# Feed-forward blocks: P6 of the first block ahead of four row casts, and the sums of gated rows behind the next quarter products' additions

## The chip, the core and the metric

The kernel runs on one core of one Trainium2 chip. The metric is device time in microseconds (us) of one execution; the kernel before takes 1314.16 us, the median of 3 runs (1312.84 to 1315.1). The engines are named as in the profile: PE is TensorE's matrix multiplication and PEld its weight loads, DVE is VectorE, ACT is ScalarE, POOL is GpSimd, SP is the engine that issues most DMAs.

## The reference

One layer of a hybrid encoder over 1024 tokens of width 1024: two attention branches, gated, and then a SwiGLU feed-forward part of hidden width 2816. All data are float32. The change touches the feed-forward part alone:

```
x = x + y @ W_out                                   # end of the attention part
h = rms_norm(x, norm_ffn)
u = silu(h @ w_gate) * (h @ w_up)                   # 2816 hidden columns = 22 blocks of 128
x = x + u @ w_down
```

## The kernel before, in words

**Three products for one.** Each float32 operand is split into a high half and a low half of the type fp32r (`split`, lines 48 to 55: a cast on ACT, line 50, then a subtraction on DVE, line 51; or, with a scale, lines 53 and 54). A product is made of three matrix multiplications, high by high, high by low and low by high: lines 823, 824 and 825.

**Seven products for eight.** Large products go through a Strassen-Winograd scheme (`Seven`). A 2 by 2 block product takes seven products P1 to P7 instead of eight, of sums of the blocks. A step P works in one of four PSUM banks of its set: P1 and P2 in bank X, P5 in V, P6 and P3 in Y, P7 and P4 in Z. There are two sets of banks, and the blocks of hidden columns take them in turn: even blocks (bankX_6627, bankY_6628, bankV_6629, bankZ_6630) and odd blocks (bankX_6631, bankY_6632, bankV_6633, bankZ_6634). After P1 ACT copies bank X into bank Y, and after P6 bank Y into bank Z (line 827), since the later products add onto those values. So P6 waits for the copy into Y, and P7 for the copy into Z. A sum of weight blocks is made on DVE (line 805), cast on ACT and completed on DVE before its product, as part of `prepare`.

**The order on the engines.** On PE the order is the order of the program everywhere. From `begin` (line 1202) to `change.close()` (line 1406) the order of ACT and DVE is also that of the program: this stretch is the passage from the attention part to the feed-forward part. Outside it a scheduler orders ACT, DVE, POOL and SP ahead of time, bound by the data and by `tc.issue_after(x)`, which keeps what is written under it behind instruction x. Each engine then works through its own list in order.

**The passage.** Blocks 0 and 1 (generators `ga` and `gb` over `hidden`, order `LAST2` = 1, 5, 6, 7, 3, 2, 4) are worked alternately while the rows of x are still being summed, split and cast (`feed`, `prepare_ffn`). After both P6, `ffn_norm` transposes the sums of squares on PE (line 1226) into the two V banks, DVE reduces them (lines 1228 and 1229), POOL takes the power -0.5 (line 1230). After both P7, `spread_norm` spreads the two results over the partitions by PE transposes (line 156), which need POOL's results. P3 follows.

**The pairs.** From block 4 on two blocks are worked as a pair. P1 of both is made together by a quarter-sized scheme of seven products (`first_products`) in the X and V banks, and parts of their P5 are worked between these products. In it DVE adds the fifth quarter product twice: into the odd block's bank X (line 1330) and into the even block's bank X (line 1333). Then ACT copies the even block's bank X into its bank Y (line 1334, on which the even block's P6 waits), and after the fourth quarter product the odd block's (line 1339). While this goes on the pair before is completed on DVE: normalised and gated (`gated`: lines 1239 to 1241; lines 1360 to 1366), and its rows u are summed for the last product (`keep` and `TokenSums`, lines 837, 840, 841 and 853, tiles ta and tb, in the profile tau and tbu), and seven tiles of a pair are stored to DRAM (line 1379, on SP). `keep` is called as the odd block of a pair is completed, in the middle of the next pair's `first_products`.

Of the kernel before, what the change touches and what calls it, by code (L numbers as in the profile page):

```python
# [25 lines left out]
def block_kernel(ctx, tc, x, xt, small, w_in, rpb, t5, w_ba, w_bb, w_out, w_gate, w_up, w_down,  # L26
                 onehot, swmask, namask, out):
    nc = tc.nc
# [196 lines left out]
    att = {}  # L225
# [205 lines left out]
    def run(gen):  # L431
        for _ in gen:
            pass
# [809 lines left out]
    us = {}  # L1243

    def quarter_rows():

        base = [temp2(f"q{z}").rearrange("p (m h t) -> p m h t", m=2, h=2) for z in "ab"]
        for j in range(4):
            dst = base[j // 2][:, j % 2]
            nc.sync.dma_start(dst, x1_dram[tok(2 * j), LO].rearrange("p (h t) -> p h t", h=2))  # L1250
        for _ in range(3):
            yield
        for j in range(4):
            dst = base[j // 2][:, j % 2]
# [12 lines left out]
        for args in ((5, t1, b12, b11, ALU.subtract), (6, t2, t1, b22, ALU.subtract),  # L1267
                     (7, b12, b12, b22, ALU.subtract), (4, b21, b21, t2, ALU.add)):
            yield
            put(*args)  # L1270
            yield
# [10 lines left out]
    def first_products(a, b):  # L1282
# [47 lines left out]
        nc.vector.tensor_add(xb[:, Q1], xb[:, Q1], p5)  # L1330
        multiply(2)
        multiply(3)
        nc.vector.tensor_add(xa[:, Q1], xa[:, Q1], p5)
        nc.scalar.copy(a.banks["Y"], xa)  # L1334
        b.step(5, (3,))
        (w[4],) = parts("d", a22, 256)
# [1 line left out]
        multiply(4)  # L1338
        att["first"] = nc.scalar.copy(b.banks["Y"], xb).ins
        yield  # L1340

    def hidden(i, order=ORDER, given=()):

        s = hid[i]
        us[i] = scratch2(f"u{i}")
        sg_lo, sg_hi = halves(us[i])
        p5, c22 = halves(scratch2(f"p5{i}"))
        y, z, v = (s.banks[b] for b in "YZV")
        for p in order:
            if p not in given:  # L1350
                s.step(p)
            if p == 2:
                gated(sg_lo, s.banks["X"], 0)
            elif p == 5:
                with ExitStack() as line:
                    if given:
                        line.enter_context(tc.issue_after(att["first"]))
                    nc.scalar.copy(p5, v)
            elif p == 7:
                att["two"] = nc.vector.tensor_add(c22, z, p5).ins  # L1360
            elif p == 3:
                nc.vector.tensor_add(sg_hi, y, p5)
                gated(sg_hi, sg_hi, 1)
            elif p == 4:
                nc.vector.tensor_mul(sg_lo, z, sg_lo)
                att["two"] = nc.vector.tensor_mul(sg_hi, c22, sg_hi).ins
                if i % 2:
                    keep(i // 2, us[i - 1], us[i])
            if p == order[3]:
                prefetch_ffn(i + 2)  # L1370
            yield p

    def keep(k, u0, u1):

        (b11, b12), (b21, b22) = halves(u0), halves(u1)
        t = TokenSums(f"u{k}", b11, b12, b22).rest(b21)
        for n, p in enumerate(ORDER):
            row = (7 * k + n) * P
            nc.sync.dma_start(u_dram[row:row + P, :], t[p][0])
# [11 lines left out]
    for i, g in enumerate((ga, gb)):  # L1391
        prepare_ffn((i, 7))
        next(g)
    add_up_ffn(4)
    feed(*((3, j) for j in range(4)))
    for i, g in enumerate((ga, gb)):
        prepare_ffn((i, 3))
        next(g)
    rs = [ffn_norm(half, sets[half]["V"]) for half in range(2)]
    feed(*((4, j) for j in range(4)))  # L1400
    both_blocks()
# [3 lines left out]
    feed(*((5, j) for j in range(4)))  # L1405
    change.close()
    in_turn(ga, gb)
    pieces = quarter_rows()
    for _ in hidden(2):
        next(pieces)  # L1410
# [5 lines left out]
    for i in range(4, NF, 2):  # L1416

        first = first_products(hid[i], hid[i + 1])
        next(first)
        run(g)  # L1420
        run(first)
        ga, g = (hidden(i + a, ORDER[1:], (5,)) for a in range(2))
        for p in ORDER[1:]:
            next(ga)
            if p != 4:
                next(g)
    run(g)

    acc = [big.tile([P, T], F32, tag="H", name=f"acc{m}", bufs=16) if m < 4 else scratch2(f"acc{m}")
           for m in range(8)]  # L1430
# [100 lines left out]
```

## Time and profile before

| what | value |
|---|---|
| median of 3 runs | 1314.16 us (1312.84 to 1315.1) |
| the profiled execution | 1314.27 us, span from first to last instruction 1312.4 us |
| PE busy in the span | 1301.0 us, 99% |
| DVE, ACT, POOL busy | 1014.9, 695.0 and 180.4 us |
| PE idle by named waits, feed-forward part | 0.9 us and 0.6 us |
| clock granted to TensorE | 1.000 |

The time of an execution is the span and what lies around it, 1.87 us here. PE is busy almost all the time, so what counts is where PE does not start its next matrix multiplication when it could. In the rows of a timeline the columns are: start in us from the span's start, duration in us, engine, line of the kernel, operation, output<-input, shape, count, and in brackets the idle time before with what ended it. A row of the chain that ended last has start, duration, engine, tile and line.

### The profile page before, as it was taken

How to read it: one execution, taken by the hardware profiler on the slowest of the kernel's cores; microseconds unless marked ns; L12 is line 12 of the kernel's file. 1: busy time of each engine (PE TensorE's matmuls, PEld its weight loads, DVE VectorE, ACT ScalarE, POOL GpSimd, SP SyncE). 2: the span in 40 equal slices, each digit the busy share in tenths (PEclk: the TensorE clock that was granted, in tenths of full speed). 3: DMA queues.
4: the chain of work that ended last, by engine and by line, in shares of the span. 5: the costliest groups of instructions: out<-in, count | busy, mean ns of one | idle time of the engine just before them, and what ended most of it. 6: DMA issues, size and time to landing. Idle time of an engine off the chain costs nothing.

```text
span 1312.4 us, 19559 instructions
## 1 busy us (share of the span) xinstructions
PE 1301.0 (99%) x6594; PEld 1130.9 (86%) x6594; DVE 1014.9 (77%) x2025; ACT 695.0 (53%) x1459; POOL 180.4 (14%) x321
## 2 busy tenths in 40 slices
PE   9999999999999999999999999999999999999998
PEld 8999999999888888888888888888888888888887
DVE  5678867776687758878999878887777799697774
ACT  7567867776664324636456544443444455363532
POOL 1364645564320000000000000000000000000000
PEclk9999999999999999999999999999999999999999
DMA  9532424242435348756774533233233356672532
GB/s 327 132 89 60 107 67 109 61 134 56 146 117 184 122 153 267 238 185 225 238 251 121 169 105 108 90 101 117 88 100 121 121 176 217 243 246 65 185 128 81
DMA packets 180997, 191.92 MB, mean 146 GB/s; under 512 B 21104, under 2 KB 126576, under 8 KB 180896
## 3 DMA queue, kind: packets, MB, share of 16 engines
q1 hardware_dynamic: 180640, 190.57, 46.3%
q8 instruction: 52, 0.85, 0.3%
q14 instruction: 49, 0.40, 0.1%
q10 hardware_dynamic: 256, 0.10, 0.0%
HBM read 133.19 MB, written 52.37 MB: 141 GB/s over the span
## 4 chain that ended last, share of the span: by engine, by line
PE 88%; DMA 5%; DVE 3%; ACT 2%; SPq 1%; issue 1%; POOL 1%; ACTq 0%; DVEq 0%; POOLq 0%
PE bankZ L823 6%; PE bankZ L824 6%; PE bankZ L825 6%; PE bankY L823 6%; PE bankY L824 6%; PE bankY L825 6%; PE bankX L823 4%; PE bankX L825 4%; PE bankX L824 4%; PE pj L324 4%; PE pj L325 4%; PE pj L326 4%; PE o L648 3%; PE bankV L824 3%; PE bankV L823 3%; PE bankV L825 3%
## 5 line engine op out<-in xcount | busy, mean ns | idle before, releaser
L602 ACT ACTIVATE E<-E,nm 128x384 f32<-128x384 f32 (+3 forms) x128 | 75.7, 592 | 47.4 <-DVE nm L596 41.3
L604 POOL TENSOR_SCALAR E<-E,nm 128x384 f32<-128x384 f32 (+1 forms) x128 | 73.4, 574 | 94.6 <-DVE nm L603 72.8
L51 DVE TENSOR_TENSOR pl<-tp,ph 128x384 fp32r<-128x384 f32 (+1 forms) x128 | 66.5, 519 | 17.6 <-ACT ph L50 16.5
L50 ACT CAST ph<-tp 128x384 fp32r<-128x384 f32 (+1 forms) x128 | 57.4, 448 | 21.3 <-PE tp L614 20.7
L50 ACT CAST f<-f 128x512 fp32r<-128x512 f32 x87 | 50.9, 620 | 23.7 <-DMA f<-u_dram 23.3
L51 DVE TENSOR_TENSOR f<-f 128x512 fp32r<-128x512 f32 x87 | 56.4, 691 | 7.1 <-ACT f L50 7.0
L614 PE MATMUL tp<-ident,E 128*128 128x128 f32 x352 | 59.5, 272 | 0.9 <-POOL E L604 0.9
L614 PEld LDWEIGHTS tp<-ident,E 128*128 128x128 f32 x352 | 45.2, 140 | 5.9 <-POOL E L604 1.2
L344 POOL TENSOR_TENSOR ss<-ss,mhalf 128x4 f32<-128x4 f32 (+2 forms) x42 | 49.7, 1182 | 3.2
L648 PE MATMUL o<-pl,v 128*128 128x256 f32 (+2 forms) x160 | 48.7, 305 | 0.9 <-DVE pl L51 0.8
L603 DVE RECIPROCAL nm<-nm 128x1 f32<-128x1 f32 x128 | 20.4, 161 | 36.8 <-ACT E L602 35.4
L648 PE MATMUL o<-ph,v 128*128 128x256 f32 (+2 forms) x160 | 45.9, 301 | 0.4 <-ACT ph L50 0.4
L590 PE MATMUL s<-k,q 128*128 128x384 f32 (+1 forms) x128 | 46.0, 359 | 0.0
L1230 POOL TENSOR_TENSOR rs<-rs,mhalf 128x4 f32<-128x4 f32 x2 | 2.2, 1105 | 318.3 <-DVE rs L1229 318.3
L591 PE MATMUL s<-k,q 128*128 128x384 f32 (+1 forms) x128 | 41.3, 323 | 0.0
L596 DVE CUSTOM_DVE_ANT_0 E<-s,bsw,cols 128x384 f32<-128x384 f32 (+1 forms) x64 | 37.0, 577 | 4.5 <-PE s L591 3.8
L1240 ACT ACTIVATE u<-u 128x512 f32<-128x512 f32 x44 | 27.5, 630 | 22.4 <-DVE u L1239 22.2
L596 DVE CUSTOM_DVE_ANT_0 E<-s,bna 128x384 f32<-128x384 f32 (+1 forms) x64 | 33.0, 517 | 4.2 <-PE s L591 3.8
L50 ACT CAST f_5h<-s1f 128x512 fp32r<-128x512 f32 x22 | 13.7, 622 | 41.7 <-DVE s1f L805 36.4
L823 PE MATMUL bankY<-f,f_6h 128*128 128x512 f32 x88 | 34.5, 392 | 0.9 <-ACT bankY L1334 0.9
L823 PE MATMUL bankZ<-f,f_7h 128*128 128x512 f32 x88 | 34.4, 390 | 0.6 <-ACT bankZ L827 0.6
L824 PE MATMUL bankV<-f,f_5h 128*128 128x512 f32 x88 | 34.4, 391 | 0.0
(1266 smaller groups left out, 4648.0 us busy)
## 6 DMA issues: line engine op xcount, KB each, us to landing
f<-u_dram SPq DMA_DIRECT2D x77, 256.0 KB
wg_s<-in_w_gate_dram SPq DMA_DIRECT2D x22, 512.0 KB
u_dram<-u SPq DMA_DIRECT2D x33, 256.0 KB
o_dram<-of SPq DMA_DIRECT2D x32, 256.0 KB
o<-o_dram SPq DMA_DIRECT2D x32, 256.0 KB
sg<-g_dram SPq DMA_DIRECT2D x32, 256.0 KB
g_dram<-go SPq DMA_DIRECT2D x24, 256.0 KB
u_dram<-tau SPq DMA_DIRECT2D x22, 256.0 KB
```

Of the source, the lines that this page charges most:

```text
L50: a = nc.scalar.copy(hi, src)
L51: b = (eng or nc.vector).tensor_tensor(lo, src, f(hi), ALU.subtract)
L324: nc.tensor.matmul(ps[:, :384], lh, his[k][:, :384], start=(k == 0), stop=False)
L325: nc.tensor.matmul(ps[:, :384], lh, los[k][:, :384], start=False, stop=False)
L596: att["bound"] = nc.vector.tensor_tensor_reduce(E[:, :n], s[:, :n], hd["bias"](qb), -1.0, sk if sw else 1e30, ALU.add, ALU.min, nm[:, 0:1] ...
L602: nc.scalar.activation(E[:, :m], E[:, :m], AF.Exp, bias=nm[:, 0:1], scale=-1.0, accum_out=nm[:, 1:2])
L604: nc.gpsimd.tensor_scalar(E[:, :n], E[:, :n], nm[:, 1:2], 1.0, op0=ALU.mult, op1=ALU.mult)
L614: nc.tensor.transpose(tp[:, tok(j)], hd["E"][qq][:, ko:ko + P], ident)
L648: nc.tensor.matmul(hd["O"][half][:, (a - half * 4) * P:(z + 1 - half * 4) * P], v[:, kb].rearrange("p a e -> p (a e)"), pp[:, (a - q0) * P ...
L823: nc.tensor.matmul(ps, hi[:, tok(j)], bh, start=first, stop=False, skip_group_check=True)
L824: nc.tensor.matmul(ps, hi[:, tok(j)], bl, start=False, stop=False, skip_group_check=True)
L825: nc.tensor.matmul(ps, lo[:, tok(j)], bh, start=False, stop=end, skip_group_check=True)
```

## The change

It has two parts. In the passage, the first block's P6, with its copy of bank Y into bank Z, is written ahead of the casts and subtractions of the rows of P3 (`feed` of `(3, j)`), and the weights of P3 are prepared for both blocks in one call after them. In the pairs, `keep` is no longer called where the odd block is completed: it is put on a list, and for the pairs in the middle it is called after the next pair's `first_products`, under `tc.issue_after(att["put"])`, where `att["put"]` is the addition of line 1333. For the first pair and the last one it is called directly after their blocks end, which is where it was.

```
--- before.py
+++ after.py
@@ -1330,7 +1330,7 @@
         nc.vector.tensor_add(xb[:, Q1], xb[:, Q1], p5)
         multiply(2)
         multiply(3)
-        nc.vector.tensor_add(xa[:, Q1], xa[:, Q1], p5)
+        att["put"] = nc.vector.tensor_add(xa[:, Q1], xa[:, Q1], p5).ins
         nc.scalar.copy(a.banks["Y"], xa)
         b.step(5, (3,))
         (w[4],) = parts("d", a22, 256)
@@ -1338,6 +1338,8 @@
         multiply(4)
         att["first"] = nc.scalar.copy(b.banks["Y"], xb).ins
         yield
+
+    done_rows = []
 
     def hidden(i, order=ORDER, given=()):
 
@@ -1365,7 +1367,7 @@
                 nc.vector.tensor_mul(sg_lo, z, sg_lo)
                 att["two"] = nc.vector.tensor_mul(sg_hi, c22, sg_hi).ins
                 if i % 2:
-                    keep(i // 2, us[i - 1], us[i])
+                    done_rows.append(lambda: keep(i // 2, us[i - 1], us[i]))
             if p == order[3]:
                 prefetch_ffn(i + 2)
             yield p
@@ -1391,11 +1393,11 @@
     for i, g in enumerate((ga, gb)):
         prepare_ffn((i, 7))
         next(g)
+    next(ga)
     add_up_ffn(4)
     feed(*((3, j) for j in range(4)))
-    for i, g in enumerate((ga, gb)):
-        prepare_ffn((i, 3))
-        next(g)
+    prepare_ffn((0, 3), (1, 3))
+    next(gb)
     rs = [ffn_norm(half, sets[half]["V"]) for half in range(2)]
     feed(*((4, j) for j in range(4)))
     both_blocks()
@@ -1405,6 +1407,7 @@
     feed(*((5, j) for j in range(4)))
     change.close()
     in_turn(ga, gb)
+    done_rows.pop()()
     pieces = quarter_rows()
     for _ in hidden(2):
         next(pieces)
@@ -1419,12 +1422,15 @@
         next(first)
         run(g)
         run(first)
+        with tc.issue_after(att["put"]):
+            done_rows.pop()()
         ga, g = (hidden(i + a, ORDER[1:], (5,)) for a in range(2))
         for p in ORDER[1:]:
             next(ga)
             if p != 4:
                 next(g)
     run(g)
+    done_rows.pop()()
 
     acc = [big.tile([P, T], F32, tag="H", name=f"acc{m}", bufs=16) if m < 4 else scratch2(f"acc{m}")
            for m in range(8)]
```

Below, the order of the engines as it is built: line, operation, output<-input with the buffers' numbers, shape. First ACT in the passage, before. Here p is the copy of a bank V, f_0 to f_2 and f_3_8046 are the row casts of P3, f_3h the casts of the two blocks' P3 weights, bankZ<-bankY the copies after P6.

```order
L1358 COPY p_8155<-bankV_6629 128x512
L50 CAST f_7h<-s3f_7954 128x512
L1358 COPY p_8170<-bankV_6633 128x512
L50 CAST f_0_8040<-f_0_8040 128x512
L50 CAST f_1_8042<-f_1_8042 128x512
L50 CAST f_2_8044<-f_2_8044 128x512
L50 CAST f_3_8046<-g22x_8104 128x512
L50 CAST f_3h<-s4f_7849 128x512
L827 COPY bankZ_6630<-bankY_6628 128x512
L50 CAST f_3h<-s4f_7955 128x512
L827 COPY bankZ_6634<-bankY_6632 128x512
```

The same place now:

```order
L1360 COPY p_8155<-bankV_6629 128x512
L50 CAST f_7h<-s3f_7954 128x512
L1360 COPY p_8170<-bankV_6633 128x512
L827 COPY bankZ_6630<-bankY_6628 128x512
L50 CAST f_0_8040<-f_0_8040 128x512
L50 CAST f_1_8042<-f_1_8042 128x512
L50 CAST f_2_8044<-f_2_8044 128x512
L50 CAST f_3_8046<-g22x_8104 128x512
L50 CAST f_3h<-s4f_7849 128x512
L50 CAST f_3h<-s4f_7955 128x512
L827 COPY bankZ_6634<-bankY_6632 128x512
```

The first block's copy (bankZ_6630) has moved ahead of four row casts and one weight cast; the second block's copy has stayed where it was. On DVE and PE nothing has moved in the passage.

Second, DVE at the pair of blocks 6 and 7, before. The tiles u_8903 and u_8906 are the rows of the pair 4 and 5, tau and tbu their sums, f_6l, f_2l and f_7l low halves of weights, s2f and s3f sums of weights, qpf the fifth quarter product. The remaining sum, line 837, stands five rows ahead of this piece.

```order
L1366 TENSOR_TENSOR u_8906<-p_8907,u_8906 128x512
L840 TENSOR_TENSOR tau_9126<-tau_9126,u_8906 128x512
L841 TENSOR_TENSOR tbu_9127<-u_8903,u_8906 128x512
L51 TENSOR_TENSOR f_6l<-s2f_9032,f_6h 128x512
L51 TENSOR_TENSOR f_2l<-wg_s,f_2h 128x512
L853 TENSOR_TENSOR tbu_9127<-u_8906,tau_9126 128x512
L1330 TENSOR_TENSOR bankX_6631<-bankX_6631,qpf_9169 128x256
L51 TENSOR_TENSOR f_2l<-wg_s,f_2h 128x512
L805 TENSOR_TENSOR s3f_9007<-wu__9002,wg_s 128x512
L1333 TENSOR_TENSOR bankX_6627<-bankX_6627,qpf_9169 128x256
L51 TENSOR_TENSOR f_7l<-s3f_9007,f_7h 128x512
```

The same place now:

```order
L51 TENSOR_TENSOR f_6l<-s2f_9032,f_6h 128x512
L51 TENSOR_TENSOR f_2l<-wg_s,f_2h 128x512
L1330 TENSOR_TENSOR bankX_6631<-bankX_6631,qpf_9156 128x256
L51 TENSOR_TENSOR f_2l<-wg_s,f_2h 128x512
L805 TENSOR_TENSOR s3f_9007<-wu__9002,wg_s 128x512
L1333 TENSOR_TENSOR bankX_6627<-bankX_6627,qpf_9156 128x256
L837 TENSOR_TENSOR tau_9220<-u_8903 128x512
L841 TENSOR_TENSOR tbu_9221<-u_8903,u_8906 128x512
L51 TENSOR_TENSOR f_7l<-s3f_9007,f_7h 128x512
L805 TENSOR_TENSOR s3f_9033<-wu__9028,wg_s 128x512
L840 TENSOR_TENSOR tau_9220<-tau_9220,u_8906 128x512
L853 TENSOR_TENSOR tbu_9221<-u_8906,tau_9220 128x512
```

The four sums have gone from ahead of the two additions into bank X (lines 1330 and 1333) to behind both of them, and the product of line 1366 (now 1368) has moved two rows ahead. The pairs 8 to 21 have the same move, with small changes beside it: on ACT one cast of the even block's f_6h stands behind the copy of line 1317, and the copies into Z stand one cast earlier. On SP the seven stores of a pair keep their place between the weight loads; among them the two of u_8906 now stand ahead of the first of tau. PE's order is the same in both kernels.

More of the change, by code (lines that the diff above doesn't have):

```diff
@@ L1332, in first_products @@
         multiply(3)
-        nc.vector.tensor_add(xa[:, Q1], xa[:, Q1], p5)
+        att["put"] = nc.vector.tensor_add(xa[:, Q1], xa[:, Q1], p5).ins
         nc.scalar.copy(a.banks["Y"], xa)
@@ L1340, in first_products @@
         yield
+    done_rows = []
     def hidden(i, order=ORDER, given=()):
@@ L1367, in hidden @@
                 if i % 2:
-                    keep(i // 2, us[i - 1], us[i])
+                    done_rows.append(lambda: keep(i // 2, us[i - 1], us[i]))
             if p == order[3]:
@@ L1393, in block_kernel @@
         next(g)
+    next(ga)
     add_up_ffn(4)
     feed(*((3, j) for j in range(4)))
-    for i, g in enumerate((ga, gb)):
-        prepare_ffn((i, 3))
-        next(g)
+    prepare_ffn((0, 3), (1, 3))
+    next(gb)
     rs = [ffn_norm(half, sets[half]["V"]) for half in range(2)]
@@ L1407, in block_kernel @@
     in_turn(ga, gb)
+    done_rows.pop()()
     pieces = quarter_rows()
@@ L1421, in block_kernel @@
         run(first)
+        with tc.issue_after(att["put"]):
+            done_rows.pop()()
         ga, g = (hidden(i + a, ORDER[1:], (5,)) for a in range(2))
@@ L1427, in block_kernel @@
     run(g)
+    done_rows.pop()()
     acc = [big.tile([P, T], F32, tag="H", name=f"acc{m}", bufs=16) if m < 4 else scratch2(f"acc{m}")
```

## The prediction

> **What bounds the kernel now.** I read the page first, then the waits of PE, then the timeline at the two places that the waits name.
>
> ```profile
> span 1312.4 us, 19559 instructions
> PE 1301.0 (99%) x6594; PEld 1130.9 (86%) x6594; DVE 1014.9 (77%) x2025; ACT 695.0 (53%) x1459; POOL 180.4 (14%) x321
> ```
>
> PE is busy in all but 11 us of the span. Its instructions and their order are the same in both kernels, so the change can only give back time in which PE stood still, or make it stand longer. These are the named waits of PE from 690 us to the end (total us, times, longest):
>
> ```profile
> PE bankY L823 <- ACT bankY L1334: 0.9, 1, 0.9
> PE bankZ L823 <- ACT bankZ L827: 0.6, 1, 0.6
> ```
>
> Two waits, once each: the first block's P7 behind its copy into Z (the first part of the change), and one even block's P6 behind its copy into Y (the second part). In the eight other pairs that copy is in time, so there the second part has nothing to win.
>
> **First part, the passage.** PE, then ACT, then DVE and POOL:
>
> ```profile
> 692.42 0.39 PE L825 MATMUL bankY<-f,f_6l 128*128 128x512 f32 x1
> ...
> 695.37 1.04 PE L1226 MATMUL bankV<-ident,wide_rs 128*128 128x128 f32 x8
> 697.00 0.50 PE L823 MATMUL bankZ<-f,f_7h 128*128 128x512 f32 x1 [0.59 <-ACT bankZ L827]
> 697.34 0.39 PE L824 MATMUL bankZ<-f,f_7h 128*128 128x512 f32 x1
> ```
> ```profile
> 693.72 1.66 ACT L50 CAST f<-f 128x512 fp32r<-128x512 f32 x3
> 695.28 0.62 ACT L50 CAST f<-g22x 128x512 fp32r<-128x512 f32 x1
> 695.84 0.62 ACT L50 CAST f_3h<-s4f 128x512 fp32r<-128x512 f32 x1
> 696.37 0.58 ACT L827 COPY bankZ<-bankY 128x512 f32<-128x512 f32 x1
> ```
> ```profile
> 696.32 1.89 DVE L51 TENSOR_TENSOR f<-f 128x512 fp32r<-128x512 f32 x3
> ...
> 698.73 1.29 DVE L51 TENSOR_TENSOR f_3l<-s4f,f_3h 128x512 fp32r<-128x512 f32 x2
> 699.93 0.69 DVE L1228 TENSOR_REDUCE rs<-bankV 128x4 f32<-128x512 f32 x1
> ...
> 700.97 2.18 POOL L1230 TENSOR_TENSOR rs<-rs,mhalf 128x4 f32<-128x4 f32 x2 [318.32 <-DVE rs L1229]
> ```
>
> P6 of block 0 ends at 692.42 + 0.39 = 692.81, so the copy is ready to go when ACT reaches it in its new place, at 693.72. It then ends at about 694.3, long before PE is through with the transposes of line 1226. PE could then go on at 696.25 (695.37 and eight steps of 0.11, the step of the four transposes below, 0.44 / 4) instead of 697.00. The first multiplication after the stand also takes 0.34 to the next, where 0.24 is the rule (807.84 to 808.08 below). Together 0.75 + 0.10 = 0.85 us at this place.
>
> The casts that the copy passes start one step of ACT later, some 0.53 (695.84 to 696.37). DVE takes the row casts only from 696.32 on, and f_3h at 698.73; in the new order the first row cast ends before 695.0, the last, of g22x, at 696.4 and the first f_3h at 697.0. So DVE is not held, and no DMA or SP instruction moves here.
>
> But what is late next? The chain that ended last goes on:
>
> ```profile
> 702.75 0.44 PE bankV L156 x4
> 703.21 0.65 PE bankV L156 x4
> ```
>
> These are the two spreads, ahead of P3 in PE's order. The second needs POOL's second power, which ends at 700.97 + 2.18 = 703.15; the spread starts 0.06 later. So it waits for POOL already now, and POOL started on DVE's reduction. DVE's order is unchanged here and it has no gap to close:
>
> ```profile
> 684.00:704.00 20.00, 19.39 (x93) 15.81 (x93) 19.90 (x34) 16.95 (x32) 2.18 (x2) 1.00 0.29 92
> 790.00:808.00 18.00, 17.06 (x95) 14.80 (x94) 17.54 (x32) 8.64 (x18) 0.00 (x0) 1.00 0.27 102
> ```
>
> (Columns: stretch, length, busy us of PE, PEld, DVE, ACT, POOL, granted clock, DMA share, GB/s.) DVE works 19.90 of 20.00 us. PE will reach the spreads 0.85 earlier, find the first result at 700.97 + 1.09 = 702.06, and stand before the second until 703.21 as before. **I count the first part as 0**; its ends are 0 and 0.85 us of gain. A loss is excluded as long as DVE is fed.
>
> **Second part, the pair of blocks 6 and 7.** PE, DVE and ACT:
>
> ```profile
> 806.16 0.28 PE L1312 MATMUL bankX<-q,qdf6h 128*128 128x256 f32 x1
> 806.28 0.28 PE L1313 MATMUL bankX<-q,qdf6l 128*128 128x256 f32 x1
> 807.51 0.50 PE L823 MATMUL bankY<-f,f_6h 128*128 128x512 f32 x1 [0.94 <-ACT bankY L1334]
> 807.84 0.40 PE L824 MATMUL bankY<-f,f_6h 128*128 128x512 f32 x1
> 808.08 0.39 PE L825 MATMUL bankY<-f,f_6l 128*128 128x512 f32 x1
> ```
> ```profile
> 797.90 0.69 DVE L837 TENSOR_TENSOR tau<-u 128x512 f32<-128x512 f32 x1
> ...
> 800.30 0.69 DVE L805 TENSOR_TENSOR s2f<-wg_s,s1f 128x512 f32<-128x512 f32 x1
> ...
> 802.84 0.69 DVE L51 TENSOR_TENSOR f_6l<-s2f,f_6h 128x512 fp32r<-128x512 f32 x1
> ...
> 804.04 0.69 DVE L853 TENSOR_TENSOR tbu<-u,tau 128x512 f32<-128x512 f32 x1
> 804.64 0.43 DVE L1330 TENSOR_TENSOR bankX<-bankX,qpf 128x256 f32<-128x256 f32 x1
> ...
> 805.58 0.69 DVE L805 TENSOR_TENSOR s3f<-wu__9002,wg_s 128x512 f32<-128x512 f32 x1
> 806.18 0.43 DVE L1333 TENSOR_TENSOR bankX<-bankX,qpf 128x256 f32<-128x256 f32 x1
> ```
> ```profile
> 801.02 0.62 ACT L50 CAST f_6h<-s2f 128x512 fp32r<-128x512 f32 x1 [1.04 <-DVE s2f L805]
> ...
> 802.07 0.36 ACT L1329 COPY bankX<-bankX 128x256 f32<-128x256 f32 x1
> ...
> 806.35 0.62 ACT L50 CAST f_7h<-s3f 128x512 fp32r<-128x512 f32 x1 [3.37 <-DVE s3f L805]
> 806.87 0.58 ACT L1334 COPY bankY<-bankX 128x512 f32<-128x512 f32 x1
> ```
>
> PE's last quarter multiplication starts at 806.28, a step of 0.12 after the one before, so the next was due at 806.40. It came at 807.51, and the one after it 0.33 later, where 0.24 is the rule: the place costs 1.11 + 0.09 = **1.20 us**. The bracket's 0.94 is less, because a multiplication's row lasts longer than its step (0.28 against 0.12); by the bracket the forecast would be 0.3 higher, and I go by the starts. The Trainium skill, "Perfetto Trace Analysis", section "Identifying the Most-Contended Engine", says that matmul busy time is a poor measure of TensorE because matmuls are pipelined, and the trace agrees here: 0.94 us of idle stand for 1.20 us of time lost.
>
> Now the new order, step by step. Four sums leave DVE ahead of line 1333, at 0.60 us a step (804.04 to 804.64): 2.4 us at most. The sum of weights at 800.30 stays there, since one sum goes from ahead of it (line 837) and one product comes (line 1366). Then DVE would be at f_6l at 800.9, but its cast ends at 801.64: f_6l at 801.7, f_2l at 802.3, line 1330 at 802.9 (its bank's copy of line 1329 ends at 802.43), s3f 0.94 later at 803.84 (804.64 to 805.58), line 1333 at 804.44 instead of 806.18. The gain is 1.74, not 2.4: 0.7 goes into waiting for the cast. ACT's cast of s3f follows s3f's start by 0.77 (805.58 to 806.35): 804.61; the copy of line 1334 by another 0.52: 805.13 to 805.71. PE starts 0.06 after the copy's end (807.45 to 807.51), so could at 805.77, and is due at 806.40. The wait goes, with 0.63 us to spare. **Gain 1.20**; its ends are 0 (the margin fails by as much as the copy was late) and 1.20.
>
> What is queued behind the held sums: f_7 and s4f on DVE, and through s4f, which frees the weight tile, the next loads on SP.
>
> ```profile
> 809.49 0.69 DVE L51 TENSOR_TENSOR f_7l<-s3f,f_7h 128x512 fp32r<-128x512 f32 x1 [1.20 <-ACT f_7h L50]
> ...
> 810.85 0.38 SPq L97 DMA_DIRECT2D wg_s<-in_w_gate_dram  x1
> ...
> 818.52 0.39 PE L823 MATMUL bankZ<-f,f_7h 128*128 128x512 f32 x1
> ```
> ```profile
> L1311 PE MATMUL bankV<-f,qaf8h x2: 278/280/283, 832.1 to 832.5; 128*128 128x256 f32 x2
> ```
>
> P7 uses f_7 from 818.52 on, over 8 us after DVE is done with it at 810.18; the sums delay it by 2.4 at most. The load at 810.85 is for the next pair, whose first multiplication with it is the row of line 1311 (durations, then first and last start): 832.1, over 20 us later, and it too is delayed by 2.4 at most. On SP the seven stores of the pair stand ahead of that load as before; those of the sums go out up to 4 us later, still ahead of the load's own release by s4f, and nothing reads them before the last product. The gated rows that the late sums read are overwritten only after the next pair's P2. So all this costs nothing, and in the other pairs the copy of line 1334 only gets earlier. Casts and copies that trade places on ACT there I put at 0 too: the copies into Z come earlier, and f_6h, one cast later, has the whole of `first_products` before its P6.
>
> **Sum.** 0 + 1.20 = 1.20 us. The profiled execution, 1314.27 us (span 1312.4), becomes 1313.07. It stands 0.11 above the median of the runs, so against the median 1314.16 I get 1312.96: **1313.0 us**, 0.09% less. A difference under 0.2% (2.6 us) is about what a measurement of this kernel cannot tell from no change.
>
> **Rivals.** (a) Both waits pay: POOL's results come earlier with the copy, and 0.85 + 1.20 = 2.05 gives 1312.1. Against it stands DVE's 19.90 of 20.00. (b) Nothing is gained: the wait behind line 1334 is only re-labelled, because line 1333 now stands behind casts instead of sums. The margin of 0.63 is thin: one more DVE step of 0.60 ahead of line 1333 nearly eats it, two leave about half of the wait, three all of it. 1314.2. (c) Slower: the held sums delay f_7 and P7 stands. This decides only where less than 2.4 us of cover is left; if all the cover were missing in each of the nine pairs, 9 x 2.4 = 21.6 on top of 1312.96 gives 1334.6; in one, 1315.4, still within 0.2%; from two on it counts as slower (1317.8). The cover of 8 us at 818.52 speaks against it. (d) A wait of PE costs more than its length, through the clock. If the 12 multiplications of a step ran at half speed after each wait, removing one would give 12 x 0.23 = 2.8 us more: 1310.2. The rows say no: 1.00 granted in both stretches, and a step of 0.24 right after the wait. The Trainium skill, "TensorE: Matmul & The Clock Gate", section "A second HAM failure mode: psum-queue depth-cycling", tells of frequent short idling between groups of matmuls that makes the clock swing; two waits in 600 us are not frequent, and no run here shows it.
>
> **How the numbers follow.** My forecast 0.70, (a) 0.08, (b) 0.13, (c) 0.05, (d) 0.02, anything else 0.02. Range: from (a) with 0.3 of scatter below, 1311.8, to (b) with as much above, 1314.5; the three runs before spread by 2.3 us, a median of three by much less. Faster by over 0.2% needs (d) or an unknown, with some scatter 0.05; slower is (c), of which most has more than one bad pair, 0.04; within 0.2% 0.91.
>
> **What would show it.** In the passage: ACT's copy into Z ahead of the row casts, P7 directly behind the transposes, and a wait of some 0.6 us before the second spread behind POOL, where there was one too short to be named. At the pair 6 and 7: line 1333 at about 804.4 and no wait before P6. If line 1230 or 1228 starts earlier, (a) is right; if a wait stands before P6 or P7 of any pair, (b) or (c).

## Result and profile after

The changed kernel takes 1316.9 us, the median of 15 runs (1313.62 to 1319.28), and the kernel before 1313.36 us beside it (15 runs, 1312.42 to 1315.1): a ratio of 1.002, 95% interval 1.0013 to 1.0027. It is slower by some 3.5 us. The forecast was 1313.0 us with a range up to 1314.5. Of all runs reported here one is left out of the ratios as slow, a run of the kernel "three sums once" below at 3391.53 us, and nothing on record explains it.

The page of the changed kernel's profiled execution (1319.28 us, the slowest of the 15: 5.01 us more than that of before and 2.4 above its own median):

```profile
span 1317.4 us, 19565 instructions
PE 1303.7 (99%) x6594; PEld 1131.4 (86%) x6594; DVE 1015.9 (77%) x2025; ACT 695.1 (53%) x1459; POOL 181.2 (14%) x321
```

The named waits of PE from 690 us on (total us, times, longest):

```profile
PE bankV L825 <- DVE d_5l L51: 2.1, 1, 2.1
PE bankX L1311 <- ACT bankX L1322: 0.7, 1, 0.7
PE bankV L156 <- POOL rs L1230: 0.7, 2, 0.5
```

The two waits of before are gone, and three others have come. They are taken in the order of time.

**The passage.** PE, ACT and POOL in the timeline:

```profile
696.15 1.03 PE L1226 MATMUL bankV<-ident,wide_rs 128*128 128x128 f32 x8
696.94 0.48 PE L823 MATMUL bankZ<-f,f_7h 128*128 128x512 f32 x1
...
702.82 0.65 PE L156 MATMUL bankV<-ident,rs 128*128 128x128 f32 x4 [0.17 <-POOL rs L1230]
703.99 0.65 PE L156 MATMUL bankV<-ident,rs 128*128 128x128 f32 x4 [0.52 <-POOL rs L1230]
```
```profile
694.50 0.59 ACT L827 COPY bankZ<-bankY 128x512 f32<-128x512 f32 x1
```
```profile
701.75 2.19 POOL L1230 TENSOR_TENSOR rs<-rs,mhalf 128x4 f32<-128x4 f32 x2 [318.18 <-ACT f_2h L50]
```

In this execution PE is already 0.78 us later than before when it reaches the transposes of line 1226 (696.15 against 695.37); that comes from the attention part, which the change does not touch. The copy into Z ends before the transposes begin, and P7 starts 0.79 after their first, without a wait. But the spreads of line 156 now wait for POOL, which is late by the same 0.78 (701.75 against 700.97). The second spread starts 7.05 us after P7 here and 6.21 before: what is won ahead of P7 is lost there.

**The pair of blocks 6 and 7.** DVE, ACT and PE:

```profile
805.01 0.42 DVE L1333 TENSOR_TENSOR bankX<-bankX,qpf 128x256 f32<-128x256 f32 x1
```
```profile
805.71 0.58 ACT L1334 COPY bankY<-bankX 128x512 f32<-128x512 f32 x1
```
```profile
807.06 0.28 PE L1313 MATMUL bankX<-q,qdf6l 128*128 128x256 f32 x1
807.18 0.40 PE L823 MATMUL bankY<-f,f_6h 128*128 128x512 f32 x1
```

P6 now follows the last quarter multiplication after one step of 0.12, where 1.23 lay between (806.28 to 807.51). The wait is gone, and 1.11 us with it; the next step is 0.10 shorter too, so that the place gives back 1.20 us by PE's starts.

**The last pair, blocks 20 and 21.** Two losses lie here. The first, 1.0 us, is at line 1311: the copy of line 1322 now stands in ACT's list behind a cast that waits 2.41 us for a sum of weights. Before, it waited for PE alone:

```profile
1064.38 0.36 ACT L1322 COPY bankX<-bankX 128x256 f32<-128x256 f32 x1 [1.69 <-PE bankX L1313]
```

And now:

```profile
1065.23 0.62 ACT L50 CAST f_6h<-s2f 128x512 fp32r<-128x512 f32 x1 [2.41 <-DVE s2f L805]
1065.75 0.37 ACT L1322 COPY bankX<-bankX 128x256 f32<-128x256 f32 x1
```

The cast stands there in every pair from blocks 8 and 9 on, and waits 2.41 us at 8 and 9 as well; there the copy ends at 838.20 and PE goes on at 838.63, so it is in time by little. In the last pair DVE is later: its first sum of the odd block waits 2.34 us for a load (0.55 to 1.33 in the pairs 8 to 19) and starts 14.6 us before PE is due at line 1311, where the other pairs have 15.6 to 16.0.

The second is the wait for d_5l. The tiles d_1 and d_5 are weights of the last product (wda1s is the stage of its second block's, loaded by SP; d_1h the cast, d_5l the low half of their sum), so the way leads from the last pair into the last product. Before, on ACT, SP, DVE and PE:

```profile
1071.55 0.62 ACT L50 CAST f_7h<-s3f 128x512 fp32r<-128x512 f32 x1 [0.93 <-DVE s3f L805]
1072.07 0.58 ACT L1339 COPY bankY<-bankX 128x512 f32<-128x512 f32 x1
...
1092.75 0.62 ACT L50 CAST d_1h<-wda1s 128x512 fp32r<-128x512 f32 x1 [3.25 <-DMA wda1s<-in_w_down_dram]
```
```profile
1086.96 0.50 SPq L97 DMA_DIRECT2D wda1s<-in_w_down_dram  x1
```
```profile
1105.43 0.69 DVE L51 TENSOR_TENSOR d_5l<-s1d,d_5h 128x512 fp32r<-128x512 f32 x1
```
```profile
1107.68 0.39 PE L825 MATMUL bankV<-f,d_5l 128*128 128x512 f32 x1
```

And now:

```profile
1072.77 0.57 ACT L1339 COPY bankY<-bankX 128x512 f32<-128x512 f32 x1 [1.84 <-PE bankX L1313]
1073.25 1.08 ACT L1360 COPY p<-bankV 128x512 f32<-128x512 f32 x2
1074.21 0.64 ACT L50 CAST f_7h<-s3f 128x512 fp32r<-128x512 f32 x1
...
1096.52 0.62 ACT L50 CAST d_1h<-wda1s 128x512 fp32r<-128x512 f32 x1 [5.42 <-DMA wda1s<-in_w_down_dram]
```
```profile
1070.88 0.60 SPq L1381 DMA_DIRECT2D u_dram<-tau  x1
...
1088.37 0.50 SPq L97 DMA_DIRECT2D wda1s<-in_w_down_dram  x1
```
```profile
1110.19 0.69 DVE L51 TENSOR_TENSOR d_5l<-s1d,d_5h 128x512 fp32r<-128x512 f32 x1
```

Before, DVE was through with d_5l at 1105.43 + 0.69 = 1106.12 and PE took it at 1107.68: a cover of 1.56 us. In the new order the cast of f_7h has fallen behind the copy of line 1339 and two more. The listing of the change does not name this move, but it stands in every pair from 8 and 9 on (there f_7h at 845.16 ahead of the copy at 845.69 before, and at 846.56 behind the copy at 845.12 now). In the last pair, all counted from P6 of block 20 (1071.84 before, 1072.57 now): s4f follows f_7h on DVE, and SP issues wda0s, the first block's weights, as s4f ends, at 3.81 us instead of 1.72; wda1s, nine row loads behind it, is issued only 0.7 us later. But it lands 3.0 us later, and d_5l comes 4.0 us later. So most of the delay in landing arises after the issue. The cover is used up, and PE stands.

The DMA engines show that transfers have moved (windows: stretch, length, busy us of PE, PEld, DVE, ACT, POOL, granted clock, DMA share, GB/s). Before:

```profile
1060.00:1070.00 10.00, 10.00 (x60) 8.85 (x59) 9.73 (x17) 3.83 (x9) 0.00 (x0) 1.00 0.73 254
1070.00:1080.00 10.00, 10.00 (x48) 8.41 (x47) 8.38 (x14) 9.07 (x19) 0.00 (x0) 1.00 0.85 281
...
1110.00:1120.00 10.00, 10.00 (x46) 8.29 (x45) 8.37 (x14) 4.67 (x8) 0.00 (x0) 1.00 0.65 230
```

Now:

```profile
1060.00:1070.00 10.00, 9.28 (x55) 7.99 (x54) 9.51 (x18) 4.60 (x10) 0.00 (x0) 1.00 0.40 141
1070.00:1080.00 10.00, 10.00 (x48) 8.38 (x48) 8.89 (x16) 8.16 (x17) 0.00 (x0) 1.00 0.96 319
...
1110.00:1120.00 10.00, 9.07 (x33) 7.32 (x34) 9.26 (x16) 3.47 (x6) 0.00 (x0) 0.83 0.43 158
```

From 1060 to 1070 the transfers run at 141 GB/s where they ran at 254, since the stores of the held sums (the row at 1070.88 is one) are not there yet; what is not moved then is moved later, ahead of the weights.

**And the clock.** The last of those rows grants PE 0.83 of its clock. PE in the timeline:

```profile
1108.42 0.40 PE L824 MATMUL bankV<-f,d_5h 128*128 128x512 f32 x1
1110.93 0.50 PE L825 MATMUL bankV<-f,d_5l 128*128 128x512 f32 x1 [2.11 <-DVE d_5l L51]
...
1112.42 0.61 PE L825 MATMUL bankV<-f,d_5l 128*128 128x512 f32 x1
1112.83 0.63 PE L823 MATMUL bankV<-f,d_5h 128*128 128x512 f32 x1
...
1115.82 0.42 PE L824 MATMUL bankY<-f,d_6h 128*128 128x512 f32 x1
```

From 1112.42 to 1115.82 a step is 0.43 us instead of 0.227: eight steps, 3.40 us in place of 1.81, 1.6 us lost. It begins 1.5 us after PE has set out again.

**The sum**, from PE's starts, for the two profiled executions: attention part +0.78, passage -0.01, pair 6 and 7 -1.20, line 1311 at the pair 12 and 13 +0.16 and at the last pair +1.00, the wait for d_5l with the slower steps around it +2.66, half clock +1.62: together +5.01, as measured. Without the attention part, which scatters from execution to execution, +4.2.

### The profile page after: what moved, and what is told of

Read it like the earlier page. It is cut to its first block, busy times and chain, and to the rows that moved or that the text cites. A ratio compares the mean times of both kernels' runs of the same rounds, so it can differ in the third digit from the quotient of the medians.

```text
span 1317.4 us, 19565 instructions
## 1 busy us (share of the span) xinstructions
PE 1303.7 (99%) x6594; PEld 1131.4 (86%) x6594; DVE 1015.9 (77%) x2025; ACT 695.1 (53%) x1459; POOL 181.2 (14%) x321
## 4 chain that ended last, share of the span: by engine, by line
PE 86%; DMA 6%; DVE 4%; ACT 2%; issue 1%; SPq 1%; POOL 1%; POOLq 0%; ACTq 0%; DVEq 0%
PE bankZ L823 5%; PE bankZ L824 5%; PE bankZ L825 5%; PE bankY L823 5%; PE bankY L824 5%; PE bankY L825 5%; PE bankX L825 4%; PE bankX L823 4%; PE bankX L824 4%; PE pj L324 4%; PE pj L325 4%; PE pj L326 4%; PE o L648 3%; PE bankV L825 3%; PE bankV L824 3%; PE bankV L823 3%
## 5 line engine op out<-in xcount | busy, mean ns | idle before, releaser
L827 ACT COPY bankZ<-bankY 128x512 f32<-128x512 f32 x42 | 24.2, 575 | 24.6 <-PE bankY L825 24.6
L1241 DVE TENSOR_TENSOR u<-u,wide_rs 128x512 f32<-128x512 f32 x44 | 30.1, 688 | 6.1 <-ACT u L1240 5.3
```

## Experiments

The theories as first put: **A**, the whole loss lies in the last pair and comes from its late stores and loads; **B**, the held sums push DVE and ACT a little further in every pair; **C**, the loss comes from the passage. Each kernel was timed in five rounds against the kernel before on the same chip.

### The last pair's sums at their old place

The edit of the changed kernel:

```
-    done_rows.append(lambda: keep(i // 2, us[i - 1], us[i]))
+    if i == NF - 3:
+        keep(i // 2, us[i - 1], us[i])
+    else:
+        done_rows.append(lambda: keep(i // 2, us[i - 1], us[i]))
```

> The changed kernel, but the sums and stores of the last held pair (blocks 18 and 19) stand at their old place. Theory A (the loss lies in the last pair alone: its seven stores, sent later, push DMA work into the stretch in which the rows and weights of the last product are loaded, these land some 4 us later, and PE stands before the last product's first P5): 1312.2 to 1312.6, below the kernel before (1313.4) by the 1.2 us won at blocks 6 and 7; no wait of PE on line 51 at the start of the last product, no half clock there. Rival B (the held sums push the chain of DVE and ACT further behind with every pair): the loss stays for the most part, 1315 to 1317. Rival C (the first part of the change, P6, makes the loss): stays at 1316.9.

Measured: 1314.99 us, ratio 1.001 (1.0001 to 1.0019). A wait of PE in its profile:

```profile
PE bankV L825 <- DVE d_5l L51: 2.3, 1, 2.3
```

The wait stays, with half clock behind it, although these sums stand where they stood. So it is not the last pair's own stores, and A as it was put is refuted. The time is close to B's, but B's losses in other pairs are not there: PE has no named wait in them. In this kernel the cast of f_7h of the last pair is seven places behind line 1339 (three in the changed kernel, one ahead of it before), and 20 loads of rows stand ahead of wda1s on SP (18, and 17 before). What reaches the last pair is an order that the earlier pairs pass on.

### Each part alone, and the last pair's sums alone

P6 alone is the kernel before with the hunk of the passage; hold alone is the changed kernel with the old passage:

```
-    next(ga)
     add_up_ffn(4)
     feed(*((3, j) for j in range(4)))
-    prepare_ffn((0, 3), (1, 3))
-    next(gb)
+    for i, g in enumerate((ga, gb)):
+        prepare_ffn((i, 3))
+        next(g)
```

Hold the last alone is the kernel before, with the list taken up behind `att["put"]` as in the change, and:

```
+    if i == NF - 3:
+        done_rows.append(lambda: keep(i // 2, us[i - 1], us[i]))
+    else:
         keep(i // 2, us[i - 1], us[i])
```

> The first part of the change alone (P6 and its copy ahead of the row casts). Theory A: 1313.4, no change: the 0.85 us won before P7 come back as a wait of PE before the spreads, which need POOL's two powers; in the profile a wait of 0.6 to 1.0 us of line 156 on line 1230. Rival C: 1316 to 1317, slower.

> The second part alone (held sums in all middle pairs, P6 as before). Theory A: as slow as the whole change, 1315 to 1318, with the wait at the start of the last product. Rival C: 1312.2, the gain at blocks 6 and 7 and no loss.

> The kernel before, with the sums of the pair 18 and 19 alone held. Theory A: the whole loss and none of the gain, 1316 to 1319, with the wait of 2 us at the start of the last product and the wait before P6 of block 6 still there. Rival B: 1313.4 to 1314.0, since one held pair cannot put the chain far behind.

Measured: P6 alone 1313.16 us, ratio 0.9994 (0.9986 to 1.0003). Hold alone 1314.99, 1.0012 (1.0003 to 1.0021). Hold the last alone 1315.31, 1.0012 (1.0004 to 1.0021), which neither theory had. The waits of P6 alone from 690 us on:

```profile
PE bankV L156 <- POOL rs L1230: 0.8, 2, 0.5
PE bankY L823 <- ACT bankY L1334: 0.8, 1, 0.8
```

C is refuted, and the forecast's first term confirmed: P7's wait has become one of the spreads, and the time is the same. The loss goes with the held sums: a wait of 1.8 us for d_5l with all of them held, of 0.8 us with the last alone. B would have losses in other pairs too; PE has no named wait there in any of these kernels. The two parts do not add up: 0.2 us less and 1.7 us more alone, 3.5 us more together. The waits for d_5l and at line 1311 are longer with both (2.1 and 0.7 against 1.8 and 0.4 with hold alone); what else makes the difference is open.

### Fewer transfers ahead of the weights

If the landing of wda1s is the cause, the changed kernel must recover when its stores or row loads are taken from in front of it.

Late stores is the changed kernel with this in `keep`; what is on the list is issued behind the row loads of the first chunk:

```
-    nc.sync.dma_start(u_dram[row:row + P, :], t[p][0])
+    if k == 9:
+        late_stores.append((row, t[p][0]))
+    else:
+        nc.sync.dma_start(u_dram[row:row + P, :], t[p][0])
```

Weights ahead is the changed kernel with this at the loads of the first chunk's rows, where `att["weights"]` is the last load of the second block's weights:

```
-    nc.sync.dma_start(f(lo), u_dram[row:row + P, :])
+    with ExitStack() as line:
+        if ch == 0 and 4 * q + j >= 12:
+            line.enter_context(tc.issue_after(att["weights"]))
+        nc.sync.dma_start(f(lo), u_dram[row:row + P, :])
```

> The changed kernel, with one thing more: the seven stores of the last kept pair (blocks 18 and 19) are issued on SP behind the row loads of the last product's first chunk instead of among them; so none of them stands ahead of the weights wda1s (7 before), and 16 row loads instead of 18. The cast of f_7h of the last pair stays where the change put it. Theory A (the loss is the landing of the last product's weights in a stretch in which the DMA queues are full): the weights are issued 1 to 2 us earlier and land in less traffic, d_1h of the second block comes at or before its place in the old kernel (20.9 us after the last pair's P6 of the even block), the wait of P5 for d_5l is gone, and with it the half clock: 1312.0 to 1313.2. Rival B (the order on ACT and DVE, f_7h three places late, makes d_5l late whatever the loads do): the wait of 1 to 2 us at P5 stays, 1314.5 to 1317.

> The changed kernel, with one thing more: the weights of the last product's second block are issued on SP behind 12 row loads instead of 18 (the stores stay ahead of them). Theory A: the weights are issued some 5 us earlier and land that much earlier, no wait at P5 for d_5l, 1312.0 to 1313.2; the rows of the first chunk come up to 1 us later and are not waited for in the first steps (if they are, a wait for f takes the place of that for d_5l, below 1 us). Rival B: unchanged against the changed kernel, a wait of 1 to 2 us at d_5l, 1314.5 to 1317.

Measured: late stores 1322.94 us, 1.0073 (1.006 to 1.0085). The weights came early (the cast d_1h 18.96 us after P6 of block 20) and d_5l was not waited for, but on DVE what empties a bank X (line 1239) fell behind row subtractions, to 1105.42: PE stood 6.3 us before the last product. The likely reason, not shown, is that the late stores hold the tiles of the last pair's sums. The test made a wait of its own and does not decide.

Weights ahead: 1314.77 us, 1.0008 (0.9999 to 1.0017), 2.1 less than the changed kernel. SP, ACT and the waits of its profile:

```profile
1087.51 0.50 SPq L97 DMA_DIRECT2D wda1s<-in_w_down_dram  x1
```
```profile
1092.62 0.62 ACT L50 CAST d_1h<-wda1s 128x512 fp32r<-128x512 f32 x1 [4.96 <-DMA wda1s<-in_w_down_dram]
```
```profile
PE bankZ L824 <- DVE p L1365: 0.7, 1, 0.7
PE bankX L1314 <- ACT bankX L1325: 0.7, 1, 0.7
PE bankY L826 <- DVE d_6l L51: 0.6, 1, 0.6
```

The wait for d_5l and the half clock are gone, though f_7h stands as late as in the changed kernel. SP issues wda1s no earlier (15.84 us after P6 of block 20 at 1071.67; 15.80 in the changed kernel), but it lands 3.0 us earlier after P6 (20.94 against 23.95): 12 loads of 256 KB lie ahead of it instead of 18. The Trainium skill, "DMA: Bandwidth & Descriptors", section "Queues, rings and completion order", says that each DMA engine takes descriptors in the order of its ring, and this agrees. The landing is not all that moved: in this kernel's lists d_5l also stands ahead of row subtractions that it stood behind, and it starts 7.0 us earlier (30.63 against 37.62). The expected 1312.0 to 1313.2 was missed: a wait for d_6l came in, that of line 1322 (here 1325) stayed, and that for p, at 756 us, is in a stretch where the lists are those of the changed kernel; there DVE stood 2.55 us for a load, 1.99 in the changed kernel.

### The cause put into the kernel before

The edit of the kernel before, which issues the second block's weights behind N of the first chunk's 28 row loads, with N = 20, 24 and 26:

```
+    if i == NF + 1:
+        return
     return prefetch_down(i - NF)
...
+    if ch == 0 and 4 * q + j == N:
+        prefetch_down(1)
     nc.sync.dma_start(f(lo), u_dram[row:row + P, :])
```

> The kernel before, with nothing of the change: only the weights of the last product's second block are issued on SP behind 20 row loads instead of 17. PE's order is the same. Theory A: the weights are issued about 2 us later and land 2 to 3 us later, more than the 1.5 us of cover that d_5l has, so the wait at P5 comes up in the kernel before as well: 1 to 2 us of wait, and up to 1.6 more where half clock follows; 1314.3 to 1316.5. Rival B: f_7h stands at its old place, so no wait, 1313.3 as before.

> The kernel before, with the weights of the last product's second block issued behind 24 row loads instead of 17 (20 took 1.05 of the 2.2 us of cover that the old order has for d_5l). At some 0.55 us a load, d_5l comes about 2.2 later than at 20: the wait at P5 is 0.8 to 1.6 us. If half clock follows only on a wait of about 2 us (waits of 0.8 to 1.1 showed none, those of 1.9 to 2.5 all did), none here: 1314.2 to 1315. Rival (late weights do not matter, the order on ACT alone makes d_5l late): 1313.4.

> The kernel before, with those weights behind 26 row loads: d_5l about 1.1 us later than behind 24, a wait of 2 to 2.7 us, and with it half clock for some 8 multiplications (1.6 us more): 1316.8 to 1318. Without half clock 1315.2 to 1316. Rival (late weights do not matter): 1313.4.

Measured: behind 20 loads 1314.03 us, 1.0003 (0.9994 to 1.0012); behind 24 1318.32, 1.004 (1.0026 to 1.0054); behind 26 1318.86, 1.0039 (1.0026 to 1.0051), the last two above what was expected. The waits in the last product, behind 24 and behind 26:

```profile
PE bankV L823 <- ACT d_5h L50: 1.3, 1, 1.3
PE bankV L825 <- DVE d_5l L51: 0.8, 1, 0.8
```
```profile
PE bankX L823 <- ACT d_1h L50: 2.2, 1, 2.2
...
PE bankV L825 <- DVE d_5l L51: 0.7, 1, 0.7
```

With nothing of the change, late weights alone make the kernel before slower by some 5 us. Behind 20 loads d_5l came 1.2 us later and the cover held; my estimate had it late, a miss. Behind 24 I expected no half clock after two waits near 1 us. The profiled execution had none, at 1315.3 us and a granted clock of 1.000, but it was the fastest of five: the others took 1317.95 to 1320.63 us at 0.997 to 0.998. So the loss through the clock is not tied to one long wait alone.

### The two gains without the late weights

Norm first is the kernel before with the passage of the change, and in it:

```
-    prepare_ffn((0, 3), (1, 3))
     next(gb)
     rs = [ffn_norm(half, sets[half]["V"]) for half in range(2)]
+    prepare_ffn((0, 3), (1, 3))
```

Three sums once is norm first, and of the pair 4 and 5 alone the sums of lines 837, 840 and 853 with the stores are taken up behind `att["put"]` of the next pair, while line 841 stays where it was. Here `keep_in_parts` makes the sums that it is given the numbers of and puts the rest, in the order of `keep`, on the list:

```
-    keep(i // 2, us[i - 1], us[i])
+    if not (i == 5):
+        keep(i // 2, us[i - 1], us[i])
+    else:
+        done_rows.append(keep_in_parts(i // 2, us[i - 1], us[i], (3,)))
```

Four sums once differs from it in one line:

```
-        done_rows.append(keep_in_parts(i // 2, us[i - 1], us[i], (3,)))
+        done_rows.append(lambda: keep(i // 2, us[i - 1], us[i]))
```

> The kernel before with the first part of the change (P6 and the copy into Z ahead of the row casts), and beside it the two reductions of the norm ahead of the two f_3l of DVE. The prediction says that the first part wins nothing because the second spread waits for POOL, which waits for DVE's reduction. If so, the reductions at 698.7 instead of 699.9 bring POOL's second result 1.2 us earlier, no wait stands at the spread, and 0.75 to 0.85 us are won: 1312.4 to 1312.7. If the f_3l, now later by two reductions and some small steps, hold P3 (due some 1 us after the spreads), the gain is 0 to 0.3: 1313.0 to 1313.4.

> P6 and its copy early as in the change, the norm's reductions ahead of the two f_3l (as in the run with the norm first), and of the held sums only three of the four of one pair (blocks 4 and 5): the pair in whose successor the wait stood. By the listing this changes the order of DVE and ACT in the pair 6 and 7 alone; in the last pair f_7h stands ahead of the copy of L1339 and 17 row loads ahead of wda1s, as in the kernel before. Theory A (the change gains what was predicted at both places, and the loss is all in the last pair): 0.8 at the passage and 1.1 at P6 of block 6 are won and nothing is lost: 1311.3 to 1311.9, no wait of PE named after 690 us. Rival B (holding sums costs somewhere else too, or the waits won come back as others): 1312.6 to 1313.6.

> As the run with three sums held once, but all four sums of that one pair are held. One sum more, and the order of ACT tips from pair to pair: in the last pair f_7h stands seven places behind the copy of L1339 and 20 row loads ahead of wda1s instead of 17. Theory A: the same two gains of 1.9 us, and in the last pair a wait for d_5l of 1.5 to 2.5 us with half clock behind it, 3.5 to 4: 1313.3 to 1315.3, and 1.7 to 3.5 more than with three sums. Rival B (the tail plays no part): the same as with three sums, within 0.5.

Measured: norm first 1313.08 us, 0.9997 (0.9988 to 1.0006). In its profile neither P7 nor a spread waits, and PE comes through the passage 1.1 us faster than before (0.84 at P7, the rest at the spreads), but the times do not show it: the 1312.4 to 1312.7 expected was missed. **Three sums once 1311.47 us, 0.9981 (0.9972 to 0.999): faster than both kernels.** Four sums once 1316.24 us, 1.0015 (1.0006 to 1.0025). Three sums once has no named wait of PE from 690 us on. PE at the pair 6 and 7, and POOL in the passage:

```profile
804.25 0.28 PE L1313 MATMUL bankX<-q,qdf6l 128*128 128x256 f32 x1
804.37 0.40 PE L823 MATMUL bankY<-f,f_6h 128*128 128x512 f32 x1
```
```profile
698.80 2.12 POOL L1230 TENSOR_TENSOR rs<-rs,mhalf 128x4 f32<-128x4 f32 x2 [316.48 <-DVE rs L1229]
```

The span, 1309.3 us, is 3.1 us shorter than that of before (some of it scatter: the medians differ by 2.0). P6 follows the quarter products after 0.12, and POOL is through with both powers at 700.92, where it was at 703.15 (0.9 us of this comes from the attention part). In the last pair all is as before (the table below).

Four sums once, its waits:

```profile
PE bankV L825 <- DVE d_5l L51: 2.4, 1, 2.4
PE bankX L1311 <- ACT bankX L1322: 0.8, 1, 0.8
```

One addition of 0.6 us more is held, in a pair 260 us earlier, and the kernel is 4.8 us slower. The lists of the two kernels are alike up to there and differ in every pair from there to the last: the order of ACT tips and stays tipped. The size was more than I expected (1.7 to 3.5).

The chain in the last pair side by side, in us after the start of P6 of block 20, read from the timelines (of the cast d_1h, which waits for the DMA, the start stands for the landing):

| kernel | f_7h cast | row loads ahead | wda1s issued | d_1h cast | d_5l starts | PE takes it |
|---|---|---|---|---|---|---|
| before | -0.29 | 17 | 15.12 | 20.92 | 33.60 | 35.84 |
| P6 alone | -0.40 | 17 | 15.12 | 20.77 | 33.52 | 35.84 |
| norm first | -0.62 | 17 | 15.12 | 21.58 | 34.26 | 35.84 |
| three sums once | -0.56 | 17 | 15.12 | 21.26 | 33.95 | 35.84 |
| before, weights behind 20 | -0.38 | 20 | 16.68 | 22.83 | 34.79 | 35.84 |
| hold the last alone | 1.63 | 18 | 15.80 | 22.48 | 36.03 | 36.77 |
| hold alone | 1.63 | 18 | 15.80 | 23.48 | 37.13 | 37.87 |
| changed kernel | 1.64 | 18 | 15.80 | 23.95 | 37.62 | 38.36 |
| last pair's sums at old place | 3.72 | 20 | 17.16 | 25.21 | 37.67 | 38.41 |
| four sums once | 3.72 | 20 | 17.16 | 25.63 | 38.00 | 38.74 |
| before, weights behind 24 | -0.57 | 24 | 22.13 | 28.19 | 37.88 | 38.61 |
| changed kernel, weights ahead | 1.64 | 12 | 15.84 | 20.94 | 30.63 | 35.84 |
| before, weights behind 26 | -0.46 | 26 | 26.20 | 31.62 | 40.30 | 41.36 |

Wherever the weights land within 2 us of their old time in an order otherwise old, PE takes d_5l at 35.84 as before. Where they land later than that it stands, whether f_7h is late or not (behind 24 and behind 26); where f_7h is late but the weights are not, it does not (last row but one). "Hold the last alone" shows that landing is not all: 1.6 us later on landing became 2.4 on d_5l, so some 0.9 us arises between the two, by the order of row casts as far as the lists tell. Among executions whose lists are alike up to there the landing itself scatters (20.77 to 21.58 in before, P6 alone, three sums once and norm first). What among the new orders pushes the landing itself, the late stores or the row loads, was not taken apart further, since the kernel with late stores made a wait of its own.

## Why the prediction was wrong

- **First part, 0: right, and for the reason given.** The second spread waits for POOL (0.5 here, some 0.6 forecast); P6 alone measured a ratio of 0.9994 (0.9986 to 1.0003). Rival (a) held that POOL's results would come earlier with the copy; they do so only if DVE's reductions are moved too.
- **Second part, 1.20 at the pair 6 and 7: right.** Line 1333 came at 805.01; taking off the 0.78 us that PE is late there, 804.23 against 804.44 forecast, P6 stands directly behind the quarter products, and PE's starts give back 1.20.
- **The step that failed** is the paragraph on what is queued behind the held sums: "So all this costs nothing", with the sentence "Casts and copies that trade places on ACT there I put at 0 too". Its covers, 8 us for f_7 and 20 us for the next loads, were read at the pair 6 and 7 and taken for all pairs. In the last pair the loads behind s4f are those of the last product, wda1s among them, in a stretch where SP and the DMA engines are filled with stores and row loads, and the cover is 1.56 us. That row stood in the trace of before and was not looked up. Two terms put at nothing there have a size: the copy of line 1322 behind the cast of f_6h cost 1.0 us at the last pair, and f_7h, which passed behind the copy of line 1339 in every pair from 8 on, is not among the trades named. The held stores were sized too small as well: "up to 4 us later" is 7.5 for the first of tau at this pair (806.06 against 798.61).
- **Rival (c), bounded too low.** Its mechanism is near to what happened, but it looked at P7 and priced one bad pair at 2.4 us, the length of the held sums. The delays at the last pair are 1.9 us on f_7h, 3.0 on the landing, 4.0 on d_5l, and so not bounded by 2.4; that the first makes the second is not shown, since with the weights ahead f_7h was as late and the landing was not. One bad pair cost 2.7 us of PE, 1.6 more by half clock and 1.0 at line 1311.
- **Rival (d), put aside on rows that did not bear on it.** They showed full clock after a wait of 1.1 us. After the wait of 2.3 us here eight steps ran at 0.43, a price of 1.6 us. That the wait removed cost no clock was right.
- **The range.** Its upper end was "nothing gained" with scatter. It had no room for a new wait, though the new order reached every later pair.

## What to carry to other kernels

A cover has to be checked at the place where it is thinnest, here the end of a loop, where the "next" loads are those of another stage, and not at the iteration where the gain lies. In a list order that a scheduler makes, a move of one operation can pass from iteration to iteration, so the two orders are best compared down to the end of the program; holding three sums in one pair kept all the gain, holding four lost it. When a wait is removed, ask what releases the engine next and move that too: the reductions here turned a wait that had only moved into 1.1 us won by PE's starts.

## What the runs showed of the hardware

Stands of PE of 2.0 to 2.6 us (by its starts) were followed, in four of the five profiled executions that had one, by 3.41 us at half rate (steps of 0.43 instead of 0.227), which began 0.8 to 1.5 us after PE had set out again; after single stands of 0.8 to 1.1 us there was none. In the fifth, four sums once, 2.55 us were followed by full steps. The 6.5 us stand of late stores brought 6.83 us at half rate, from 3 us before its end on. The Trainium skill, "TensorE: Matmul & The Clock Gate", section "Part 1: The HAM clock gate", says that the clock halves after at least one idle window of about 3.4 us, and that the window runs freely. The length of the slow stretch agrees with that window; but here shorter stands were enough, in some executions and not in others.

The clock records of the traces show what separates them. In all 14 the clock changes only at whole multiples of 3.413 us from the first record of full rate (in the changed kernel at 1112.43, 324 of them after 6.52), so that each execution falls into windows whose borders lie elsewhere in the program. In the window just ahead of the half rate PE was busy 1.50, 1.45, 1.58 and 1.39 of 3.41 us in the four (changed kernel, last pair's sums at old place, hold alone, behind 26). In four sums once a border cut the stand in two, at 1108.00: PE was busy 1.90 and 2.53 us in the two windows, and both were followed by full rate; so were 2.14 and 2.64 us behind 24. Until PE is done, the only other windows under 1.90 us are two of late stores, 0.08 and 0.45, and half rate followed both. So in these traces half rate follows a window in which PE is busy for less than about half, and the same stand can bring it or not by where the border falls. No run was made to test this. In this kernel, where PE is busy 99% of the time, a wait of 2 us thus had a price of up to 1.6 us beside its own length. That would make runs of one kernel scatter, and those of the changed kernel do: 1313.62 to 1319.28 us.
